# Filters' loop of a hybrid attention and Hyena kernel: token transpositions moved and paired, a fourth PSUM bank from the eighth step

## The chip, the cores and the metric

One core of one Trainium2 chip. The metric is the time of an execution in microseconds, as the device reports it; three runs of the kernel before took 1793.38, 1794.36 and 1795.69 us. One further execution was taken with the profiler: 1791.72 us, of which 1789.9 us are the span that the trace covers. The change touches one loop, which takes about a tenth of the span.

## The reference, cut to what matters

The reference is a backbone of two layers over 1024 latent tokens and 256 context tokens of width 1024: an attention layer, then a Hyena layer, then a final RMSNorm.

```
h_lat = rms_norm(x_lat, norm_w[0]) * (1 + scale) + shift        # 1024 tokens
h_ctx = rms_norm(x_ctx, norm_w[0]) * (1 + scale_c) + shift_c    # 256 tokens
attention over h_lat, h_ctx: (h @ w_in) split into queries, keys, values, gate ...
# odd layer
h    = sin-MLP(positions) @ w3 + b3, times exp(-t * |deltas|)   # filters: 2 orders, 2 directions, 1024 channels
kern = [fwd, 0, reversed bwd];  kern = kern / sum |kern|
k_f  = rfft(kern)                                               # the spectrum that the long convolutions multiply by
```

The loop that is changed does two things that do not depend on each other. It computes the filters' spectrum k_f for the Hyena layer (by two stages of matrix products in place of an FFT), and in its gaps it prepares the attention layer's input: each of 10 tiles of 128 tokens (2 of context, 8 latent) is scaled by its reciprocal norm, transposed, modulated, and split into a high and a low part for products of nearly full precision.

## The kernel before

Instructions of TensorE (PE), VectorE (DVE), ScalarE (ACT) and GpSimd (POOL) are written out by hand: each engine runs them in the order of the program text. DMA issues on SyncE (SP) are not: their order is made when the kernel is built, by when buffers are expected free, and an issue can stand far ahead of its place in the text.

The filters' loop (L615) has 38 steps, n = 0 to 37. Steps 0 to 31 each take one of 32 parts (8 groups p of 128 channels, 4 parts each); the later stages trail behind: the first stage one step (`first_stage(n - 1, .)`), the second stage and the copies of spectra six steps. In the text a step is, in order:

- `taps(n)`: eight products into a two-bank PSUM tile `pw` (L483, L484)
- `second_stage(.., 0)`: products of the regrouped first-stage results `au` (L583) into one bank `pq`
- `decayed(n)`: DVE multiplies the taps by the decay, tile `kern` (L541)
- `decay(n + 1, .)`: ACT's exponentials for the next step (L536), whose one buffer `dec` is free when `kern` is done
- `spectra(.., 0)`: DVE scales the second stage's bank into `kc` (L594), and a DMA stores it to `Kd`
- `first_stage(n - 1, 0 and 1)`: a product of `sum` or `dif` (L568) and ACT's copy to `aT` (L569), one half after the other, the decays between them
- `halves(n)`: GpSimd's sum and difference of `kern`'s halves (L561); `norms(n)`: DVE's reduction of absolute values `kabs` (L548) and GpSimd's addition (L552)
- `second_stage(.., 1)`, `regroup` (DMAs from `aT` to `au`, L578), `spectra(.., 1)`: the second `kc`
- every fourth step: the sum over partitions (L649) and its reciprocal `rn` (L661), n = 5, 9, 13, ...; the split of the next coefficients (`split_coefs`: L345 and L348 on ACT, L346 on GpSimd, L349 on DVE), n = 2, 6, 10, ...
- at the end of a step, generators are pulled: `row_stats` (the tiles' norms, up to step 11), then `xprep` (the tokens, steps 11 to 32), and `first_products` (steps 32 to 35).

`xprep` (L392) handles half a tile (four blocks of 128 columns) per step. One pull issues four transpositions into a bank `pq` (L414); the next, directly behind, issues four activations on ACT that scale and shift into `raw` (tile `mraw`, L419), the castings to the high part on DVE (L426) and the subtractions that give the low part on GpSimd (L427). Context tiles have one 128x512 casting per half, latent tiles two of 128x256. At the start of a tile DVE scales all of it (L408), every second step, and the next tile's load is issued (L399), into one of two `xt` buffers.

`pq()` hands out PSUM banks in rotation: a product waits until the reader of the bank's last use is done. At first three banks rotate, since the fourth, "c", serves the modulation's products early in the loop; it is put into the rotation at the end of step 19.

`first_products` are the first blocks of the attention layer's input projection: 12 products of 128x288 per pull. Their weights are loaded at step W1N = 22 into the buffer `ckh`, split at step 24 into `ckl` and `kpe` (L678 on ACT, L679 on GpSimd), and the next part of the weights is loaded into `ckh` at step 26 (L682). In the last group of channels the stores of `kc` are issued by ACT. Behind the loop the remaining first products and all other chunks of the projection follow; their weights are split on ACT (L742) and GpSimd (L743), and ACT's part stands in its queue behind the stores of `kc`.

The token section's core, of before:

```
            nc.vector.tensor_scalar(xt, xt, rr[:, t:t + 1], 0.0, ALU.mult, ALU.add)
            load()
            for k0 in (0, 4):
                yield
                ps = pq()
                for i in range(4):
                    nc.tensor.transpose(ps[:, i * P:(i + 1) * P], xt[:, (k0 + i) * P:(k0 + i + 1) * P], ident)
                yield
```

Of the kernel before, what the change touches and what calls it, by code (L numbers as in the profile page):

```python
# [9 lines left out]
F32 = mybir.dt.float32  # L10
# [7 lines left out]
P = 128  # L18
# [22 lines left out]
W1N = 22  # L41
HP = {32: 1, 33: 1, 34: 1, 35: 1}
# [62 lines left out]
def f(ap):  # L105
    return ap.bitcast(F32)


def backbone(tc, I, out):
# [12 lines left out]
    def nm(s):  # L122
        cnt[0] += 1
        return f"{s}_{cnt[0]}"
# [9 lines left out]
    def pq():  # L134

        t = banks.popleft()
        banks.append(t)
        return bank(t)
# [253 lines left out]
    def xprep():  # L392

        xts = []

        def load():
            if len(xts) < NC + NT:
                xt = pre.tile([P, D], F32, tag="xt", bufs=2, name=nm("xt"))
                nc.sync.dma_start(xt, xsrcs[len(xts)])  # L399
                xts.append(xt)  # L400

        load()
        yield
        for t in range(NC + NT):
            who, t0 = ("x", t * P) if t < NC else ("l", (t - NC) * P)
            A, Sh = ada[who, 0, "scale"], ada[who, 0, "shift"]
            xt = xts[t]
            nc.vector.tensor_scalar(xt, xt, rr[:, t:t + 1], 0.0, ALU.mult, ALU.add)  # L408
            load()
            for k0 in (0, 4):  # L410
                yield
                ps = pq()
                for i in range(4):
                    nc.tensor.transpose(ps[:, i * P:(i + 1) * P], xt[:, (k0 + i) * P:(k0 + i + 1) * P], ident)  # L414
                yield
                raw = pre.tile([P, 4, P], F32, tag="mraw", bufs=2, name=nm("mraw"))
                for i in range(4):
                    k = k0 + i
                    nc.scalar.activation(raw[:, i], ps[:, i * P:(i + 1) * P], AF.Identity, bias=Sh[:, k:k + 1], scale=A[:, k:k + 1])  # L419
                if who == "x":  # L420
                    dst = [((hxh[:, k0:k0 + 4, t0:t0 + P], hxl[:, k0:k0 + 4, t0:t0 + P]), raw)]
                else:
                    th, c = divmod(t0, 512)
                    dst = [([h0[th, k0 // 2 + j, i][:, :, c:c + P] for i in range(2)], raw[:, 2 * j:2 * j + 2]) for j in range(2)]
                for (hi, lo), r in dst:
                    nc.vector.tensor_copy(hi, r)  # L426
                    nc.gpsimd.tensor_tensor(lo, r, f(hi), ALU.subtract)  # L427
# [7 lines left out]
    def pull(g, n=1):  # L435
        for _ in range(n):
            next(g, None)
# [3 lines left out]
    with tc.manual_schedule(engines=ENG):  # L441
# [173 lines left out]
        for n in range(N + 6):  # L615
# [9 lines left out]
            pb, ub = divmod(n - 6, 4)  # L625
            if 0 < n < N:
                taps(n)
            if n >= 6:
                ps0 = second_stage(pb, ub, 0)
            if n < N:  # L630
                decayed(n)
            decay(n + 1, 0)
# [7 lines left out]
            if n < N:  # L640
                halves(n)
                norms(n)
            if n >= 6:
                ps1 = second_stage(pb, ub, 1)
# [29 lines left out]
            if 12 < n < 33:  # L674
                pull(toks, 2)
            if n == W1N + 2:
                for k in range(4):
                    nc.scalar.copy(w0[1][:, k], w0[0][:, k])  # L678
                    nc.gpsimd.tensor_tensor(w0[2][:, k], w0[0][:, k], f(w0[1][:, k]), ALU.subtract)  # L679
            if n == W1N + 4:  # L680
                w1 = ckp.tile([P, KEYS], F32, tag="ckh", bufs=1, name=nm("w0"))[:, :4 * 288].rearrange("p (k n) -> p k n", k=4)
                nc.sync.dma_start(w1, win[:, 4:8, 0:288])  # L682
            pull(first_products, HP.get(n, 0))
            if n == 19:
                banks.append("c")
# [1628 lines left out]
```

## Time and profile before

| what | value |
|---|---|
| three runs | 1793.38, 1794.36, 1795.69 us |
| profiled execution | 1791.72 us |
| its span in the trace | 1789.9 us |
| steps 12 to 31 of the loop, start of kern to start of kern | 95.65 to 223.80 us of the span |
| tail of the loop | about 229 to 251 us |
| busy share of the span | PE 95%, DVE 63%, POOL 47%, ACT 42% |

A row of the order of time gives start and length in microseconds, the engine ("q" behind it: its queue of DMA issues), the line, the operation, what it writes and reads, the shape, and a count when equal ones follow each other; in brackets stands how long the engine sat idle before it and what ended that. A grouped row gives the count, the busy time in us and the mean in ns of one, and the idle time before them with what ended it. Lengths of neighbours on DVE overlap by some 0.08 us, so sums are made from start to start.

### The profile page before, as it was taken

The page shows a single profiled execution, that of the slowest core. Times are in us where ns is not written, and L with a number is a line of the kernel's source. Part 1 is how long each engine was busy: PE and PEld are TensorE (multiplying, and loading weights), DVE is VectorE, ACT ScalarE, POOL GpSimd, SP SyncE. Part 2 cuts the span into 40 slices and gives each one's busy share as a digit, 9 for nine tenths or more (in the row PEclk, how much of TensorE's full clock was granted, in tenths as well). Part 3 has the DMA queues.
Part 4 walks back from the last instruction along what each step waited for, and adds up shares of the span by engine and source line. Part 5 has one row for each costly group of instructions (what it writes and reads, how often), then busy time and mean ns, then how long its engine had stood idle before and what let it go on. Part 6 is the DMA issues. An engine that isn't in the chain of part 4 may idle for free. (4 is left out here: it accounts for less than half of the span.)

```text
span 1789.9 us, 25447 instructions
## 1 busy us (share of the span) xinstructions
PE 1698.6 (95%) x9360; PEld 1313.9 (73%) x9360; DVE 1136.4 (63%) x1625; ACT 751.7 (42%) x1293; POOL 837.1 (47%) x612
## 2 busy tenths in 40 slices
PE   6888899998999999999999999999999999999898
PEld 2555588986766666666666788888888888878786
DVE  6888957636666665466665324556777667756843
ACT  4766621243545545644444333233333333333331
POOL 3667832524179877677777453123222223233300
PEclk8999999999999999999999999999999999999999
DMA  7776787322220010100010226456776666686432
GB/s 258 243 217 200 211 260 266 110 71 72 57 57 28 11 44 14 52 31 24 22 34 22 78 94 161 138 152 203 199 213 174 196 201 196 196 231 181 155 108 104
DMA packets 237372, 236.48 MB, mean 132 GB/s; under 512 B 30575, under 2 KB 195223, under 8 KB 236831
## 3 DMA queue, kind: packets, MB, share of 16 engines
q1 hardware_dynamic: 235072, 232.76, 43.6%
q10 hardware_dynamic: 2176, 2.10, 0.4%
q8 instruction: 74, 1.21, 0.3%
q14 instruction: 50, 0.41, 0.1%
HBM read 152.87 MB, written 61.94 MB: 120 GB/s over the span
## 5 line engine op out<-in xcount | busy, mean ns | idle before, releaser
L1010 DVE TENSOR_REDUCE mx<-pq 128x1 f32<-128x512 f32 x256 | 170.9, 682 | 100.4 <-PE pq L1009 98.6
L1315 ACT ACTIVATE PT<-pw 128x1024 f32<-128x1024 f32 x160 | 163.6, 1025 | 166.1 <-PE pw L1297 160.1
L100 PE MATMUL pw<-h1h,wh 128*128 128x512 f32 x512 | 208.4, 407 | 0.0
L102 PE MATMUL pw<-h1h,wl 128*128 128x512 f32 x512 | 201.3, 393 | 0.0
L101 PE MATMUL pw<-h1l,wh 128*128 128x512 f32 x512 | 200.0, 391 | 0.0
L1209 POOL TENSOR_TENSOR acc<-acc,PT 128x1024 f32<-128x1024 f32 x62 | 147.4, 2378 | 20.4 <-ACT PT L1315 18.9
L1733 POOL TENSOR_TENSOR wl<-wr,wh 128x1024 fp32r<-128x1024 f32 x32 | 77.1, 2409 | 137.8 <-ACT wh L1732 127.5
L102 PEld LDWEIGHTS pw<-h1h,wl 128*128 128x128 f32 x512 | 96.1, 188 | 21.3
L101 PEld LDWEIGHTS pw<-h1l,wh 128*128 128x128 f32 x512 | 96.5, 188 | 17.7
L100 PEld LDWEIGHTS pw<-h1h,wh 128*128 128x128 f32 x512 | 96.5, 188 | 17.4
L1868 POOL TENSOR_TENSOR K<-K,skp 128x512 f32<-128x512 f32 x32 | 42.7, 1337 | 122.7 <-DMA K<-Kd 121.7
L1207 POOL TENSOR_TENSOR acc<-PT,PT 128x1024 f32<-128x1024 f32 x31 | 74.0, 2386 | 52.5 <-ACT PT L1315 49.8
L1881 DVE TENSOR_TENSOR cA<-pq,K 64x512 f32<-64x512 f32 x128 | 88.1, 689 | 1.8
L1877 DVE SCALAR_TENSOR_TENSOR cB<-pq,K 64x512 f32<-64x512 f32 x64 | 44.4, 693 | 70.4 <-PE pq L1874 35.6
L1848 ACT COPY caT<-pq 128x512 f32<-128x512 f32 x64 | 37.6, 588 | 118.1 <-PE pq L102 98.1
L583 PE MATMUL pq<-au,FBk 128*128 128x256 f32 x256 | 71.6, 408 | 14.8 <-DVE kc L594 11.1
L1894 PEld LDWEIGHTS pq<-cA,GB 128*128 128x128 f32 x512 | 67.3, 193 | 15.3 <-issue 10.3
L1200 PE MATMUL pv<-PT,Va 128*64 128x256 f32 x640 | 77.9, 385 | 0.0
L1896 ACT COPY cbT<-pq 128x512 f32<-128x512 f32 x64 | 37.5, 587 | 95.7 <-PE pq L1894 67.1
L1200 PE MATMUL pv<-PT,Vm 128*64 128x256 f32 x640 | 77.7, 385 | 0.0
L1894 PE MATMUL pq<-cA,GB 128*128 128x128 f32 x512 | 68.8, 278 | 7.9 <-DVE cA L1884 6.9
L1911 DVE TENSOR_TENSOR cil<-spare,cih 128x512 fp32r<-128x512 f32 x64 | 53.8, 879 | 34.8 <-ACT cih L1910 34.6
(448 smaller groups left out, 4672.6 us busy)
## 6 DMA issues: line engine op xcount, KB each, us to landing
au<-aT SPq DMA_DIRECT2D x128, 128.0 KB
space<-in_ada_w_dram SPq DMA_DIRECT2D x32, 512.0 KB
wr<-in_hy_w_in_dram SPq DMA_DIRECT2D x32, 512.0 KB
K<-Kd SPq DMA_DIRECT2D x64, 256.0 KB
ad<-caT SPq DMA_DIRECT2D x64, 256.0 KB
cau<-ad SPq DMA_DIRECT2D x32, 512.0 KB
bd<-cbT SPq DMA_DIRECT2D x32, 512.0 KB
spare<-bd SPq DMA_DIRECT2D x64, 256.0 KB
```

What stands on the lines that cost most here:

```text
L100: nc.tensor.matmul(ps, lh, rh, start=start, stop=False)
L101: nc.tensor.matmul(ps, lh, rl, start=False, stop=False)
L102: nc.tensor.matmul(ps, ll, rh, start=False, stop=stop)
L583: nc.tensor.matmul(ps[:, i * CB:(i + 1) * CB], FBk[:, 4 * uc + 2 * j + i, :], aus[p, uc][:, 2 * j + i, :], start=True, stop=True)
L1010: nc.vector.reduce_max(m[:, i, j:j + 1], ps, axis=AX.X)
L1200: nc.tensor.matmul(ps[64 * e:64 * e + 64, 0:256], vals[:, 2 * s + j], PT[:, j, 256 * e:256 * e + 256], start=s == 0 and j == 0, stop=s == ...
L1207: eng.tensor_tensor(accs[gi], prev, PT, ALU.add)
L1209: eng.tensor_tensor(accs[gi], accs[gi], PT, ALU.add)
L1315: nc.scalar.activation(PT, ps.rearrange("p (a q) -> p a q", q=512), AF.Exp, scale=SC_A if kind == 0 else SC_M)
L1733: nc.gpsimd.tensor_tensor(wl, f(r), f(wh), ALU.subtract)
L1881: nc.vector.tensor_tensor(A1[64 * e:64 * e + 64], pv[64 * e:64 * e + 64], K[:, 0], ALU.mult)
L1894: nc.tensor.matmul(ps[:, i * P:(i + 1) * P], GB[:, 4 * uc + i, :], A1[:, i, :], start=True, stop=True)
```

## The change

`xprep` works on pairs of tiles. A step now takes two blocks of 128 columns of both tiles of a pair: four transpositions into one bank, two activations of 128x256, one casting and one subtraction of 128x512, for context and latent tiles alike. The work of a step is pulled in four pieces at four places of its text: the transpositions ahead of the taps; the activations behind kern and ahead of the next decays; casting and subtraction behind the halves and ahead of the norms; and, behind the norms, once per pair, the next loads and the scaling of the next two tiles. In DVE's queue the casting so stands between the first kc and kabs, and the scalings between kabs and the second kc.

The loads are no longer two buffers deep. Five tiles are asked for at step 11, and three of the ten go through `ckh`, `ckl` and `kpe`, two more through `ckl` and `kpe` later. The first weights therefore move: their load is written at step 26 in place of 22, their split at step 32 (24), the second load at step 34 (26), and the first products are pulled in steps 33 to 36 (32 to 35). The bank "c" joins the rotation at the end of step 6 in place of 19.

```
-W1N = 22
-HP = {32: 1, 33: 1, 34: 1, 35: 1}
+W1N = 26
+XT = ("xt", "xt") + CK + ("xt", "xt", "ckl", "xt", "kpe")
+LN = 2, 1, 2, 0, 0
+HP = {33: 1, 34: 1, 35: 1, 36: 1}
...
+        def scaled(t):
+            for i in range(t, min(t + 2, NC + NT)):
+                nc.vector.tensor_scalar(xts[i], xts[i], rr[:, i:i + 1], 0.0, ALU.mult, ALU.add)
+
+        load(5)
         yield
-        for t in range(NC + NT):
+        scaled(0)
+        yield
+        for t in range(0, NC + NT, 2):
...
+            for k0 in range(0, NK, 2):
+                ps = pq()
+                for k in range(2):
+                    for i in range(2):
+                        nc.tensor.transpose(ps[:, (2 * k + i) * P:(2 * k + i + 1) * P], xts[t + i][:, (k0 + k) * P:(k0 + k + 1) * P], ident)
                 yield
+                raw = pre.tile([P, 4, P], F32, tag="mraw", bufs=2, name=nm("mraw")).rearrange("p (k i) c -> p k (i c)", k=2)
+                for k in range(2):
+                    kk = k0 + k
+                    nc.scalar.activation(raw[:, k], ps[:, 256 * k:256 * k + 256], AF.Identity, bias=Sh[:, kk:kk + 1], scale=A[:, kk:kk + 1])
                 yield
...
+                nc.vector.tensor_copy(hi, raw)
+                nc.gpsimd.tensor_tensor(lo, raw, f(hi), ALU.subtract)
+                yield
+                if k0 == NK - 2:
+                    load(LN[t // 2])
+                    scaled(t + 2)
+                yield
...
+            tokens = 12 < n < 33
+            if tokens:
+                pull(toks)
             if 0 < n < N:
                 taps(n)
             if n >= 6:
                 ps0 = second_stage(pb, ub, 0)
             if n < N:
                 decayed(n)
+            if tokens:
+                pull(toks)
             decay(n + 1, 0)
...
             if n < N:
                 halves(n)
+            if tokens:
+                pull(toks)
+            if n < N:
                 norms(n)
+            if tokens:
+                pull(toks)
...
-            if 12 < n < 33:
-                pull(toks, 2)
-            if n == W1N + 2:
+            if n == W1N + 6:
...
-            if n == W1N + 4:
+            if n == W1N + 8:
...
-            if n == 19:
+            if n == 6:
                 banks.append("c")
```

`load(n_)` issues the next n_ tiles' loads, each into the buffer that `XT` names.

More of the change, by code (lines that the diff above doesn't have):

```diff
@@ L394, in xprep, with load @@
         xts = []
[L396 to L399, printed above, removed]
+        def load(n_):
+            for t in range(len(xts), min(len(xts) + n_, NC + NT)):
+                tag = XT[t]
+                xt = (pre.tile([P, D], F32, tag=tag, bufs=2, name=nm("xt")) if tag == "xt" else
+                      ckp.tile([P, KEYS], F32, tag=tag, bufs=1, name=nm("xt"))[:, :D])
+                nc.sync.dma_start(xt, xsrcs[t])
@@ L400, in load @@
                 xts.append(xt)
-        load()
+        def scaled(t):
+            for i in range(t, min(t + 2, NC + NT)):
+                nc.vector.tensor_scalar(xts[i], xts[i], rr[:, i:i + 1], 0.0, ALU.mult, ALU.add)
+        load(5)
         yield
-        for t in range(NC + NT):
+        scaled(0)
+        yield
+        for t in range(0, NC + NT, 2):
             who, t0 = ("x", t * P) if t < NC else ("l", (t - NC) * P)
             A, Sh = ada[who, 0, "scale"], ada[who, 0, "shift"]
[L407 to L410, printed above, removed]
+            for k0 in range(0, NK, 2):
[3 more added lines that the diff above has]
+                        nc.tensor.transpose(ps[:, (2 * k + i) * P:(2 * k + i + 1) * P], xts[t + i][:, (k0 + k) * P:(k0 + k + 1) * P], ident)
@@ L411, in xprep @@
                 yield
-                ps = pq()
-                for i in range(4):
-                    nc.tensor.transpose(ps[:, i * P:(i + 1) * P], xt[:, (k0 + i) * P:(k0 + i + 1) * P], ident)
+                raw = pre.tile([P, 4, P], F32, tag="mraw", bufs=2, name=nm("mraw")).rearrange("p (k i) c -> p k (i c)", k=2)
+                for k in range(2):
+                    kk = k0 + k
+                    nc.scalar.activation(raw[:, k], ps[:, 256 * k:256 * k + 256], AF.Identity, bias=Sh[:, kk:kk + 1], scale=A[:, kk:kk + 1])
@@ L415, in xprep @@
                 yield
[L416 to L419, printed above, removed]
                 if who == "x":
-                    dst = [((hxh[:, k0:k0 + 4, t0:t0 + P], hxl[:, k0:k0 + 4, t0:t0 + P]), raw)]
+                    hi, lo = (x[:, k0:k0 + 2, t0:t0 + 256] for x in (hxh, hxl))
@@ L422, in xprep @@
                 else:
                     th, c = divmod(t0, 512)
[L424 to L427, printed above, removed]
+                    hi, lo = (h0[th, k0 // 2, i][:, :, c:c + 256] for i in range(2))
+                nc.vector.tensor_copy(hi, raw)
+                nc.gpsimd.tensor_tensor(lo, raw, f(hi), ALU.subtract)
```

## The prediction

> **What bounds the kernel now.** I read the page first, then the filters' loop in windows of four steps (one group of 128 channels: the loop repeats with that period), then the groups of instructions inside it, and at last the order of time of VectorE and GpSimd.
>
> ```profile
> span 1789.9 us, 25447 instructions
> ```
>
> The windows below are cut at starts of the row "kern" (L541), one per step: steps 14 to 17, 18 to 21, 22 to 25, 26 to 29, and then the tail from the first product of step 32 to the first product behind the loop. The columns are the length, then busy time (count) of PE, PEld, DVE, ACT and POOL, the granted clock, the DMA share and GB/s.
>
> ```profile
> 107.72:136.07 28.35, 23.99 (x99) 16.64 (x100) 23.21 (x27) 17.19 (x46) 19.47 (x18) 0.88 0.67 195
> 136.07:163.63 27.56, 23.65 (x101) 16.16 (x102) 24.29 (x30) 17.00 (x46) 20.30 (x22) 0.94 0.69 205
> 163.63:190.86 27.23, 23.57 (x100) 15.72 (x101) 25.14 (x30) 18.14 (x50) 23.35 (x26) 0.94 0.69 202
> 190.86:217.55 26.69, 22.24 (x99) 15.16 (x98) 24.64 (x31) 16.83 (x46) 20.29 (x22) 0.94 0.71 214
> 228.75:251.36 22.61, 22.37 (x136) 20.37 (x135) 10.58 (x15) 3.53 (x9) 3.70 (x6) 1.00 0.85 245
> ```
>
> In the loop DVE is busy 23.2 to 25.1 of about 27 us and is the engine that the others wait for. In the tail PE is busy 22.37 of 22.61: there PE sets the end, and behind it the products go on without a pause, so what the loop and the tail gain or lose is what the kernel gains or loses.
>
> VectorE, from the middle of step 26 to the start of step 28 (start, length, engine, line, operation; in brackets the idle time before it and what ended it):
>
> ```profile
> 194.53 0.68 DVE L594 TENSOR_TENSOR kc<-pq,rn 128x512 f32<-128x512 f32 x1
> ...
> 196.74 0.53 DVE L349 TENSOR_TENSOR WB<-b3r,WB 1x256 fp32r<-1x256 f32 x1 [0.33 <-ACT WB L348]
> 197.44 0.29 DVE L426 CAST h<-mraw 128x256 fp32r<-128x256 f32 x1 [0.17 <-ACT mraw L419]
> ...
> 198.67 0.74 DVE L408 TENSOR_SCALAR xt<-xt,rr 128x1024 f32<-128x1024 f32 x1
> 199.33 1.21 DVE L541 TENSOR_TENSOR kern<-pw,dec 128x1024 f32<-128x1024 f32 x1
> ```
>
> ```profile
> 200.47 0.68 DVE L594 TENSOR_TENSOR kc<-pq,rn 128x512 f32<-128x512 f32 x1
> 201.06 2.02 DVE L548 TENSOR_REDUCE kabs<-kern 128x256 f32<-128x1024 f32 x1
> 203.00 0.68 DVE L594 TENSOR_TENSOR kc<-pq,rn 128x512 f32<-128x512 f32 x1
> 203.60 0.45 DVE L426 CAST h<-mraw 128x256 fp32r<-128x256 f32 x1
> 204.30 0.70 DVE L426 CAST h<-mraw 128x256 fp32r<-128x256 f32 x1 [0.25 <-ACT mraw L419]
> 204.92 1.21 DVE L541 TENSOR_TENSOR kern<-pw,dec 128x1024 f32<-128x1024 f32 x1
> ```
>
> From start to start, step 27 spends 1.14 on kern, 0.59 on the first kc, 1.94 on kabs, 0.60 on the second kc, 4.27 in all, and then 1.32 on two token castings. Step 26 has the castings from 197.27 (their wait included) to 198.67, 1.40. The same stretch on GpSimd:
>
> ```profile
> 200.69 1.28 POOL L561 TENSOR_TENSOR sum<-kern 128x512 f32<-128x512 f32 x1 [0.69 <-DVE kern L541]
> 201.92 1.29 POOL L561 TENSOR_TENSOR dif<-kern 128x512 f32<-128x512 f32 x1
> 203.16 0.73 POOL L552 TENSOR_TENSOR kabs<-kabs,kabs 128x256 f32<-128x256 f32 x1
> 204.13 0.73 POOL L427 TENSOR_TENSOR h<-mraw,h 128x256 fp32r<-128x256 f32 x1 [0.23 <-DVE h L426]
> ```
>
> This is what the forecast rests on. A casting with GpSimd idle takes 0.29 (197.44). The one at 203.60 meets the running kabs sum, which ends at 203.89, and ends 0.16 behind it; the one at 204.30 meets a subtraction that ends at 204.86 and ends 0.14 behind it. A casting that starts while a GpSimd operation runs does not end before that operation has. The kabs reduction (201.06) runs beside both halves and takes its usual time.
>
> **The change part by part.**
>
> *Castings.* Forty tile halves become twenty blocks of 128x512, one per step: 36 castings become 20. What a double one costs with GpSimd idle is the second row here, and the first the present form with its waits in:
>
> ```profile
> L426 DVE CAST h<-mraw 128x256 fp32r<-128x256 f32 x30 | 12.5, 429 | 5.1 <-ACT mraw L419 5.1
> L426 DVE CAST hxh<-mraw 128x512 fp32r<-128x512 f32 x4 | 1.6, 411 | 3.9 <-ACT mraw L419 3.9
> L427 POOL TENSOR_TENSOR hxl<-mraw,hxh 128x512 fp32r<-128x512 f32 x4 | 5.9, 1477 | 7.8 <-DVE hxh L426 7.8
> ```
>
> The waits for ACT (5.1 and 3.9) go, because transposition and activation now stand a good part of a step ahead. But the casting now stands behind the first kc, at the place of 201.06, where the sum half runs until 201.97. It then ends about 0.28 later (0.16 as above and 0.12 for the double width), at 202.25, and kabs can start at 202.17: 1.11 us per step where 0.41 would be the cost with GpSimd idle. Bounds: 0.34 (0.41 less the usual overlap of starts) and 2.4 (it also loses its turn to the dif half, 1.29). I take 1.11.
>
> *Scalings.* Before, one tile every second step at 0.74; now two at once every fourth step, behind kabs. GpSimd's queue has then sum, dif (pushed to 202.2 to 203.5) and the low parts, 1.48 wide form, until about 205; kabs ends near 204.1. If a scaling waits like a casting, the first ends at about 205.5, the kabs addition (0.73) takes its turn, and the second ends near 206.7: 2.6 for the pair. If not, 2 x 0.74 = 1.48. These are the bounds, and I take 2.6, since it is the castings' case. [...] No scaling of the trace of before starts under a running GpSimd operation.
>
> *Other parts of a cycle.* The reciprocal stays, 1.76. The coefficients' split waits for ACT's chain, which hangs on kern: its second part starts at 196.74, 5.88 behind that step's kern (190.86). Now the second kc starts at 3.67 + 1.11 = 4.78 and ends its turn at 5.38, the split ends at about 6.4 as before: 1.1 instead of 2.1 (195.13 to 197.27). So the later kc is hidden in this one step of four. A cycle: 4 x 4.27 + 4 x 1.11 + 1.76 + 2.6 + 1.1 = 27.0. The four cycles measured make 109.83; four of 27.0 make 108: **-1.8**, nearly all in the first cycle.
>
> *Transpositions first.* The same 80 on PE, moved ahead of the taps. PE has 22.2 to 24.0 us of work in a cycle of 27, so they cost nothing while DVE is this slow; below 24 PE would be next. Activations: two of 128x256 instead of four of 128x128; ACT is busy 17 of 27. Hidden by kern's wait, in either form. The low parts: one of 1.48 for two of 0.73, GpSimd is busy 20 of 27, hidden.
>
> *Fourth bank from step 7.* It can only take away waits of PE for kc and of DVE for PE. Of these DVE felt
>
> ```profile
> 71.26 1.23 DVE L541 TENSOR_TENSOR kern<-pw,dec 128x1024 f32<-128x1024 f32 x1 [0.64 <-PE pw L484]
> ```
>
> ```profile
> L583 PE MATMUL pq<-au,FBk 128*128 128x256 f32 x256 | 71.6, 408 | 14.8 <-DVE kc L594 11.1 <-ACT mraw L419 2.5 <-DMA au<-aT 1.2
> ```
>
> The first row is worth **-0.6** (0 to -0.9); PE's waits for kc, in the second, are idle time of an engine that is not the bound there.
>
> *Loads.*
>
> ```profile
> 44.77 0.38 SPq L624 DMA_DIRECT2D w<-in_w_in_dram  x1
> ```
>
> SP issues as soon as a buffer is free, not in step order: the weight load written at step 22 went out at 44.77. So the three token tiles in ckh, ckl and kpe go out there as well, 1.5 MB instead of 0.58; at 240 to 260 GB/s that is 4 us more in the queue ahead of the first au. PE waited 1.2 us for au in the whole loop: cost 0 (to 3). Scaling now needs tiles 0 and 1 at the end of step 12:
>
> ```profile
> 98.12 0.40 SPq L596 DMA_DIRECT2D Kd<-kc  x1
> 98.62 0.41 SPq L399 DMA_DIRECT2D xt<-in_ctx_dram  x1
> ...
> 99.84 0.74 DVE L408 TENSOR_SCALAR xt<-xt,rr 128x1024 f32<-128x1024 f32 x1
> ...
> 102.50 0.69 DVE L594 TENSOR_TENSOR kc<-pq,rn 128x512 f32<-128x512 f32 x1 [0.79 <-DMA Kd<-kc]
> ```
>
> The second scaling adds **+0.7**. The store issued at 98.12 frees its buffer at 102.5, so tile 1, issued behind it at 98.62, lands near 102.9; DVE wants it at 100.5. If its place in SP's queue stays, that is a wait of 2.4; if it moves up with its step, 0. I take **+1.0**.
>
> *Tail.*
>
> ```profile
> 228.22 1.10 PE L568 MATMUL pq<-dif,FKc 128*128 128x512 f32 x2 [0.18 <-DVE kc L594]
> 230.38 0.38 PE L100 MATMUL pw<-w,hxh 128*128 128x288 f32 x1
> 232.05 1.89 PE L583 MATMUL pq<-au,FBk 128*128 128x256 f32 x8
> 239.53 1.97 PE L583 MATMUL pq<-au,FBk 128*128 128x256 f32 x8 [0.24 <-DMA au<-aT]
> ```
>
> The last first-stage product waits for the last kc (0.18), which now stands behind a casting: up to 0.9 later. One block of first products (230.38 to 232.05, 1.67) no longer fills the wait for au ahead of 239.53: PE comes there 1.67 earlier and waits up to that much more. And the second weight load (576 KB; 2.4 us at 245 GB/s), which used to pass in the loop, now goes out when the split of step 32 is done, among the last au. Bounds 0 and 4.9; I take **+2.5**.
>
> Sum: -1.8 - 0.6 + 0.7 + 1.0 + 2.5 = **+1.8 us**. The profiled execution took 1791.72 around its span of 1789.9, so 1793.5; the median of the runs, 1794.36, lies 2.64 above that execution, so **1796.2** is what I expect of a median. Own range of this case 1793 to 1801.
>
> **The rivals.**
>
> *A. The castings do not wait for GpSimd* (they slip in ahead of the sum half, or the sum starts late). Then a casting costs 0.41, the scalings 1.48, and a cycle 4 x 4.68 + 1.76 + 1.48 + 2.1 = 24.1, which is just above PE's work. That is 2.9 less in each of four cycles and some 0.8 in the last steps: 1796.2 - 12.4 = 1784. For it: the waits for ACT do end, and two of the four steps have no other use for the time. Against it: every casting above that met a GpSimd operation ended behind it, and the sum starts 0.15 behind kern each time.
>
> *B. The tail decides* (slower). Here the loop comes out as forecast, but the second weight load passes in front of the last au and the missing block adds its full time: +4.9 instead of +2.5, with tile 1's full wait of 2.4: 1796.2 + 3.8 = 1800; with au late at the loop's start too, 1803. It decides from the point where PE idles over 2 us between step 32 and the first product behind the loop. For it: DMA is at 0.85 there, the highest of the five windows. Against it: SP may hold the load back.
>
> *C. The castings wait for both halves*, 2.4 each: 20 x 1.29 = 26 more, 1822; in one step of four, 1803. Against it: 203.60 ended right behind one operation.
>
> *D. Nothing changes* because VectorE's sum of work is the same and all else is hidden: 1794.
>
> **How the numbers follow.** Forecast 0.45, A 0.27, B 0.15, C 0.08, D 0.05. A measurement of this kernel can tell about 0.2%, 3.6 us, from no change. Faster by more: nearly all of A and a little of the forecast's lower end, 0.29. Slower by more: a third of the forecast, most of B and C, 0.35. Between: 0.36. The range from 1781 to 1804 takes in A, B, and C where it is rare.
>
> **What would show it.** In the new profile the casting (x20, 128x512) starts inside the sum half and lasts near 1.1 us, not 0.41; the waits for ACT ahead of it are gone; the scalings' pairs take 2.6; the step with the split is shorter, that with the reciprocal longer; a cycle is near 27; PE idles more between step 32 and the chunk. [...]

## The result, and the profile after

The changed kernel takes 1806.76 us (median of 5, 1806.32 to 1811.29), the kernel before in the same comparison 1793.38 us: the comparison puts the ratio at 1.009, 95% interval 1.0071 to 1.0109 (the two medians alone give 1.0075). It is slower by 13.4 us where I forecast 1796.2, and outside my range. The profiled spans stand 1804.9 to 1789.9, so the traces have 15.0 us to account for.

The same cut into cycles of four steps as in the prediction, at kern of steps 13, 17, 21, 25 and 29 (length, then busy time of PE, PEld, DVE, ACT and POOL, granted clock, DMA share, GB/s), in the changed kernel:

```profile
106.84:135.49 28.65, 23.05 (x99) 16.32 (x98) 25.87 (x25) 15.12 (x38) 19.26 (x17) 0.92 0.63 192
135.49:163.73 28.24, 22.71 (x99) 15.89 (x98) 25.84 (x25) 15.12 (x38) 19.26 (x17) 0.92 0.64 190
163.73:192.56 28.83, 23.22 (x99) 16.03 (x98) 25.93 (x26) 15.12 (x38) 19.26 (x17) 0.91 0.62 193
192.56:221.22 28.66, 23.06 (x99) 16.16 (x98) 25.88 (x25) 15.12 (x38) 19.27 (x17) 0.92 0.57 165
```

I had forecast 27.0. DVE is busy 25.9 and PE 23, so neither is full: in each cycle DVE stands still for more than 2 us. VectorE in order of time, step 16 and the start of step 17, shows where:

```profile
126.22 1.21 DVE L553 TENSOR_TENSOR kern<-pw,dec 128x1024 f32<-128x1024 f32 x1
127.35 0.68 DVE L606 TENSOR_TENSOR kc<-pq,rn 128x512 f32<-128x512 f32 x1
127.95 1.17 DVE L433 CAST hxh<-mraw 128x512 fp32r<-128x512 f32 x1
129.05 1.92 DVE L560 TENSOR_REDUCE kabs<-kern 128x256 f32<-128x1024 f32 x1
130.87 1.82 DVE L408 TENSOR_SCALAR xt<-xt,rr 128x1024 f32<-128x1024 f32 x2
132.61 0.68 DVE L606 TENSOR_TENSOR kc<-pq,rn 128x512 f32<-128x512 f32 x1
135.49 1.22 DVE L553 TENSOR_TENSOR kern<-pw,dec 128x1024 f32<-128x1024 f32 x1 [2.20 <-PE pw L496]
```

kern waits 2.20 for the taps (pw). TensorE over the same moment shows why the taps are late:

```profile
132.18 0.30 PE L421 MATMUL pq<-ident,xt 128*128 128x128 f32 x1 [3.77 <-DVE xt L408]
...
133.30 0.56 PE L495 MATMUL pw<-WA,HA 128*128 128x256 f32 x1
133.66 0.41 PE L496 MATMUL pw<-WB,HB 128*128 128x256 f32 x1
133.87 0.41 PE L495 MATMUL pw<-WA,HA 128*128 128x256 f32 x1
```

The transpositions of step 17 are first in PE's queue and wait 3.77 for a tile that VectorE scales only at the end of step 16. The taps need nothing from that tile, but they stand behind it, and kern needs the taps. So VectorE waits for PE, which waited for VectorE. The same wait stands at kern of step 13, behind the first scalings, and of steps 21, 25 and 29:

```profile
102.64 1.40 DVE L408 TENSOR_SCALAR xt<-xt,rr 128x1024 f32<-128x1024 f32 x2
106.84 1.22 DVE L553 TENSOR_TENSOR kern<-pw,dec 128x1024 f32<-128x1024 f32 x1 [2.80 <-PE pw L496]
...
163.73 1.23 DVE L553 TENSOR_TENSOR kern<-pw,dec 128x1024 f32<-128x1024 f32 x1 [2.20 <-PE pw L496]
...
192.56 1.22 DVE L553 TENSOR_TENSOR kern<-pw,dec 128x1024 f32<-128x1024 f32 x1 [1.80 <-PE pw L496]
...
221.22 1.22 DVE L553 TENSOR_TENSOR kern<-pw,dec 128x1024 f32<-128x1024 f32 x1 [2.20 <-PE pw L496]
```

With step 17 that is 11.2 us.

The whole difference, in sections cut at kern's starts and at the first product behind the loop (PE `pw<-wh,hxh`, 251.36 before), in us:

| from | to | before | after | difference |
|---|---|---|---|---|
| kern 1 | kern 6 | 23.9 | 24.9 | +1.0 |
| kern 6 | kern 11 | 31.1 | 32.9 | +1.9 |
| kern 11 | kern 13 | 10.2 | 13.6 | +3.5 |
| kern 13 | kern 31 | 123.3 | 126.1 | +2.8 |
| kern 31 | first product | 27.6 | 32.6 | +5.0 |
| first product | end | 1538.6 | 1539.3 | +0.8 |

The first row need not be the change: two kernels below that are the kernel before in these steps take 24.9 and 24.8 there, and five variants with the changed kernel's text there take 23.9 to 24.3.

### The profile page after: what moved, and what is told of

Its sections match the earlier page's. It is cut to its first block, busy times and chain, and to the rows that moved or that the text cites. A ratio compares the mean times of both kernels' runs of the same rounds, so it can differ in the third digit from the quotient of the medians.

```text
span 1804.9 us, 25367 instructions
## 1 busy us (share of the span) xinstructions
PE 1703.1 (94%) x9360; PEld 1317.9 (73%) x9360; DVE 1138.5 (63%) x1609; ACT 742.1 (41%) x1253; POOL 831.3 (46%) x596
```

## The experiments

Theory Q, formed from the comparison above: the taps, queued behind transpositions that wait for a late scaling, cost the loop's gain and more; the castings cost what I had forecast; early loads and the tail make up the rest. Rivals: the castings or the loads set the time and the wait is only where it shows; the tail comes from late stores and not from the weights. The same sections in all kernels, with the ratio to the kernel before as each one's own comparison gives it ("product" is the first product behind the loop, which the expectations also call the first product of the second half):

| kernel | 6 to 11 | 11 to 13 | 13 to 31 | 31 to product | product at | ratio |
|---|---|---|---|---|---|---|
| before | 31.1 | 10.2 | 123.3 | 27.6 | 251.4 | |
| after | 32.9 | 13.6 | 126.1 | 32.6 | 265.5 | 1.0090 |
| a_taps_first | 34.5 | 10.8 | 121.8 | 31.9 | 258.7 | 1.0053 |
| a_scale_early | 32.7 | 13.7 | 122.3 | 32.2 | 260.4 | 1.0055 |
| a_cast_late | 34.0 | 14.3 | 120.3 | 31.5 | 259.5 | 1.0043 |
| a_tf_cl | 33.3 | 10.8 | 111.9 | 31.9 | 247.3 | 1.0004 |
| a_both | 32.5 | 13.6 | 119.5 | 30.5 | 255.2 | 1.0040 |
| a_load_late | 29.8 | 15.0 | 130.1 | 32.1 | 267.3 | 1.0087 |
| a_loads | 30.9 | 13.2 | 126.9 | 32.3 | 262.6 | 1.0073 |
| b_bank6 | 31.2 | 10.1 | 121.0 | 27.8 | 250.2 | 1.0000 |
| b_tail | 30.9 | 10.2 | 121.5 | 31.0 | 253.8 | 1.0008 |
| b_hp33 | 30.1 | 10.2 | 122.3 | 29.4 | 251.4 | 1.0009 |
| b_w1late | 31.0 | 10.2 | 121.8 | 30.3 | 252.9 | 1.0027 |
| c_best | 31.2 | 13.1 | 112.1 | 31.8 | 247.4 | 0.9985 |
| c_w1_32 | 32.2 | 13.2 | 111.3 | 31.0 | 247.7 | 0.9991 |
| c_w1_34 | 28.5 | 14.9 | 115.1 | 31.2 | 249.9 | 0.9987 |

What follows the first product took 1537.0 to 1544.4 us in these profiles, without a pattern I can name; so sections are read from the traces, and ratios only where they are clear of that. A section of a single profile varies too, where the text is the same: steps 13 to 31 take 123.3 in the kernel before and 122.3 in b_hp33, which is the same there (121.0 to 121.8 in the other b kernels); steps 6 to 11 take 32.5 to 34.5 in the changed kernel and the five variants with its early loads, and 28.5 to 32.2 in the three c kernels. So a difference below 2 us between two profiles in these two sections, and below 4 in the c kernels' steps 6 to 11, is not told from chance.

### The queue: a_taps_first and a_scale_early

```diff
-            if tokens:
-                pull(toks)
             if 0 < n < N:
                 taps(n)
             if n >= 6:
                 ps0 = second_stage(pb, ub, 0)
+            if tokens:
+                pull(toks)
```

> The changed kernel, but a step's four transpositions stand behind its taps and its first second-stage product on TensorE; castings, bank, loads and scaling as changed. Theory Q (queue): the taps stood behind transpositions that wait for the scaling, which VectorE does at the end of the step before; so the product kern of steps 13, 17, 21, 25 and 29 no longer waits for the taps (2.80, 2.20, 2.20, 1.80 and 2.20 us in the changed kernel, 11.2 in all). Of that some 0.77 us per cycle comes back, because the casting of those steps then meets GpSimd's sum again (1.19 us instead of 0.42): about -7 us, 1800 us (1797 to 1802). Rival C (castings and loads set the time, the wait only shows where VectorE is early): steps 13 to 31 keep their length, 1805 to 1808 us.

Measured: 1801.87 us, ratio 1.0053 (1.0037 to 1.0069). No kern waits for taps any more; the three full cycles from step 17 on, by the same columns:

```profile
133.07:159.81 26.74, 21.58 (x100) 14.35 (x100) 26.54 (x27) 15.22 (x38) 19.49 (x17) 1.00 0.70 201
159.81:187.60 27.79, 22.93 (x100) 15.82 (x99) 26.86 (x27) 14.99 (x38) 19.46 (x17) 0.94 0.68 204
187.60:214.33 26.73, 21.57 (x100) 14.36 (x99) 26.53 (x26) 15.11 (x38) 19.48 (x17) 1.00 0.61 176
```

DVE is busy 26.5 of 26.7: it is the bound again. TensorE in step 17 of this kernel:

```profile
129.47 0.28 PE L496 MATMUL pw<-WB,HB 128*128 128x256 f32 x1
129.59 0.28 PE L495 MATMUL pw<-WA,HA 128*128 128x256 f32 x1
...
132.04 0.30 PE L421 MATMUL pq<-ident,xt 128*128 128x128 f32 x1 [1.19 <-DVE xt L408]
```

The transposition still waits for the scaling, 1.19, but now nothing that VectorE needs soon stands behind it. The first product behind the loop comes 6.8 us earlier. Rival C (castings and loads) falls for these 7 us.

```diff
+                if k0 == NK - 4:
+                    scaled(t + 2)
                 if k0 == NK - 2:
                     load(LN[t // 2])
-                    scaled(t + 2)
```

> The changed kernel, but a pair of token tiles is scaled one step earlier (at the end of the third step of a cycle of four, not of the fourth); the transpositions stay first on TensorE, everything else as changed. Theory Q (queue): the scaling is a whole step ahead of the transposition that needs it, so kern of steps 17, 21, 25 and 29 no longer waits for the taps (2.20, 2.20, 1.80, 2.20 = 8.4 us; step 13's 2.80 stays), 0.77 us of each comes back by a longer casting: about -5.5 us, 1801 us (1798 to 1804). Rival C (castings and loads): the scaling only changes places, 1805 to 1808 us. Rival O (order alone): even a ready transposition ahead of the taps delays kern; waits of over 1 us stay and the time is 1804 to 1807 us.

Measured: 1801.59 us, ratio 1.0055 (1.0039 to 1.0071); the waits at steps 17, 21, 25 and 29 are gone, that of step 13 (2.80) stands, the product comes 5.2 us earlier. Transpositions ahead of the taps make no kern wait where their tile is ready, so rival O falls too: what cost these 8.4 us of waits is the late input at the head of TensorE's queue.

### The castings: a_cast_late

```diff
             if n < N:
                 halves(n)
-            if tokens:
-                pull(toks)
-            if n < N:
                 norms(n)
...
                 spectra(pb, ub, 1, ps1)
+            if tokens:
+                pull(toks)
```

(In the token generator the scaling goes ahead of the casting, so that it keeps its place.)

> The changed kernel, but the casting of a step (with its low part) stands at the end of VectorE's step, behind the second spectrum copy, where GpSimd has done its sum; transpositions, scaling, bank and loads as changed. Theory L (the casting pays for GpSimd's running sum): the 14 castings of 1.17 to 1.22 us come down to about 0.45, some -10 us; the waits of kern for the taps stay, and the scaling is followed by one casting more, so they are shorter rather than longer: 1797 us (1794 to 1801). Rival W (the width of the casting is its price): it stays at 1.2 us, 1805 to 1809 us. Rival P (TensorE sets the cycle): castings of 0.45 us but the waits of kern grow by as much, 1804 to 1808 us.

Measured: 1799.65 us, ratio 1.0043 (1.0025 to 1.0062). A casting of the changed kernel and GpSimd's sum beside it, in order of time on each engine:

```profile
115.04 1.27 POOL L573 TENSOR_TENSOR sum<-kern 128x512 f32<-128x512 f32 x1 [1.01 <-DVE kern L553]
115.41 1.19 DVE L433 CAST hxh<-mraw 128x512 fp32r<-128x512 f32 x1
137.28 0.42 DVE L433 CAST h<-mraw 128x512 fp32r<-128x512 f32 x1
```

The casting starts inside the sum, which ends at 116.31, and ends at 116.60, 0.29 behind it; the one at 137.28, in a step where kern and so the sum were late, took 0.42. With the casting at the end of the step, where only the short kabs sum runs:

```profile
126.09 0.72 POOL L564 TENSOR_TENSOR kabs<-kabs,kabs 128x256 f32<-128x256 f32 x1
126.43 0.67 DVE L437 CAST hxh<-mraw 128x512 fp32r<-128x512 f32 x1
```

All but one of the twenty castings now take 0.41 to 0.67. Width is not the price (rival W), the GpSimd instruction that happens to run is. The taps' waits stayed (2.81, 1.87, 1.58, 1.54, 0.74), so rival P falls.

### Both moves: a_tf_cl and a_both

a_tf_cl has the edits of a_taps_first and a_cast_late, a_both those of a_scale_early and a_cast_late.

> Both moves at once: the transpositions behind the taps and the first second-stage product, and the casting at the end of VectorE's step; scaling, bank, loads and tail as in the changed kernel. Theory Q with L: with the transpositions moved alone a steady cycle of four steps is 26.9 us (152.78 to 179.69), all of it VectorE at work; four castings of some 0.55 instead of 1.19 us take 2.5 off: cycles of 24.4 us, the stretch from kern of step 13 to kern of step 31 some 111 us (121.8 with the transpositions moved alone, 123.3 before), 1789 us (1786 to 1793), so a little faster than the kernel before. Rival P (TensorE, or the Kd stores, become the bound below 26 us): waits for PE or for DMA show up at kern or kc, the stretch stays above 117 us and the time is 1794 to 1798 us.

Measured: the section from 13 to 31 is 111.9 us, as theory Q with L has it (111), against 123.3 before. Its cycles:

```profile
129.91:154.56 24.65, 21.30 (x99) 14.35 (x98) 23.32 (x27) 15.13 (x39) 19.01 (x17) 1.00 0.74 222
154.56:180.13 25.57, 21.24 (x99) 14.35 (x98) 23.37 (x26) 14.98 (x39) 18.98 (x17) 1.00 0.72 213
180.13:204.22 24.09, 21.05 (x99) 14.35 (x98) 23.40 (x27) 15.13 (x39) 19.02 (x17) 1.00 0.71 222
```

So the change's own parts, in another order on two queues, take 11.4 us off steps 13 to 31 (9.1 against the shortest b kernel). The time is 1792.23 us, ratio 1.0004 (0.9989 to 1.002), that of the kernel before and above the 1789 I expected: the start and the tail keep 7.1 us of it (2.2, 0.6 and 4.3 in the table's sections), and behind the first product, which comes 4.1 us earlier than before, the profile is 2.3 us longer, which I cannot explain.

> The scaling one step earlier and the casting at the end of VectorE's step; the transpositions stay first on TensorE, all else as in the changed kernel. Theory Q with L: with the scaling moved alone a steady cycle is 27.5 us (154.93 to 182.49), in which the scaled pair takes 2.23 us and the castings 1.2; with castings of some 0.55 it is 25 us; kern of step 13 still waits 2.8 us: 113 to 115 us from kern of step 13 to kern of step 31, 1791 us (1788 to 1795). Rival O (a transposition ahead of the taps costs of itself, since it waits for what the step before does last): the waits of kern for the taps come back at over 0.5 us, 1795 to 1800 us.

Measured: 1798.1 us, ratio 1.004 (1.0026 to 1.0055), and 119.5 us for the section: my figure was too low, and by neither theory: the time lies in rival O's range, but its sign, waits of kern, stayed away. No kern but that of step 13 waits for taps; kc waits for its stores instead, on VectorE, as here in step 16:

```profile
132.85 0.69 DVE L607 TENSOR_TENSOR kc<-pq,rn 128x512 f32<-128x512 f32 x1 [2.84 <-DMA Kd<-kc]
```

and SP shows two token loads, 1 MB, just ahead of the stores:

```profile
123.72 0.95 SPq L403 DMA_DIRECT2D xt<-in_x_dram  x2
125.34 0.38 SPq L609 DMA_DIRECT2D Kd<-kc  x1
128.12 0.38 SPq L609 DMA_DIRECT2D Kd<-kc  x1
```

With cycles near 25 us the bunching of transfers may be the next limit; that these two loads are the cause was not tried by itself.

### The early loads: a_load_late

```diff
+                if t in (2, 3, 4):
+                    nc.vector.memset(xt[:, 0:1], 0.0)
                 nc.sync.dma_start(xt, xsrcs[t])
```

> The changed kernel, but the loads of token tiles 2, 3 and 4 can't start before step 11: VectorE writes a zero into the first column of each buffer there, and the load has to come behind it; all else as changed. Theory B (burst): the three loads at 45.8 and 49.7 us make the statistics' tiles and the first regrouping loads late; kern of step 6 to kern of step 11 takes 31.1 to 31.7 us as in the kernel before (31.09) and with the bank alone (31.21), instead of 32.9 to 34.5 in the changed kernel and its three variants: 1.3 to 3 us less, 1804.5 us (1802 to 1806.5). Rival: the steps 6 to 10 come out over 32.7 us again, and it is the later scaling or the statistics themselves; 1806 to 1808 us.

Measured: 1807.49 us, ratio 1.0087 (1.007 to 1.0103). In the changed kernel SP issues

```profile
45.76 0.38 SPq L403 DMA_DIRECT2D xt<-in_x_dram  x1
48.70 0.33 SPq L381 DMA_DIRECT2D xs<-in_x_dram  x1
49.72 0.83 SPq L403 DMA_DIRECT2D xt<-in_x_dram  x2
53.98 2.93 SPq L590 DMA_DIRECT2D au<-aT  x4
```

and with the three token loads held back steps 6 to 11 take 29.8 us instead of 32.9: theory B is right for this section. But five loads then go out together at 92.6 to 97.0, PE waits for au in step 13,

```profile
107.96 2.05 PE L597 MATMUL pq<-au,FBk 128*128 128x256 f32 x4 [2.89 <-DMA au<-aT]
```

and the later sections lose 5.3 us (11 to 31). The burst was moved, not spread, and the time is that of the changed kernel, as the rival had it.

### The bank: b_bank6

```diff
-            if n == 19:
+            if n == 6:
                 banks.append("c")
```

> The kernel before with one edit: the fourth bank is used from the eighth step instead of from the twenty-first. By the steps of the two traces (steps 7 and 8: 4.94 and 5.13 us before, 4.22 and 4.45 in the changed kernel) it takes 1.4 us from these two steps and some tenths from the later ones: 1791.5 us (1790 to 1793). Rival: the short steps come from what was late ahead of them and not from the bank: within 0.1% of the kernel before, steps 7 and 8 as before.

Measured: 1792.98 us, ratio 1.0 (0.9988 to 1.0013). kern's wait of 0.64 at 71.26 is gone and steps 7 and 8 take 9.14 instead of 10.07 us, but steps 9 and 10 take 1.0 more, and step 6 to 11 comes out as before (31.2 and 31.1). TensorE waits there for a regrouping load, which an earlier start does not bring sooner:

```profile
83.59 1.10 PE L583 MATMUL pq<-au,FBk 128*128 128x256 f32 x4 [3.66 <-DMA au<-aT]
```

I had expected 1.4 and more to remain; the rival was right on the time, though steps 7 and 8 did change.

### The tail: b_tail, b_hp33 and b_w1late

In the kernel before, the weights' part of the change:

```diff
-HP = {32: 1, 33: 1, 34: 1, 35: 1}
+HP = {33: 1, 34: 1, 35: 1, 36: 1}
-            if n == W1N + 2:
+            if n == W1N + 10:
-            if n == W1N + 4:
+            if n == W1N + 12:
```

> The kernel before with the weights' part of the change alone: the first weights are split at the end of step 32 instead of 24, the second load of weights stands behind step 34 instead of 26, and the first half of the products starts in step 33 instead of 32; tokens, castings and bank as before. Theory T (missing filler and a late second load): from kern of step 31 to the first product of the second half takes 31.5 to 32.5 us, as in the changed kernel and its variants (31.5 to 32.6), instead of 27.6 before: 1796.5 us (1795 to 1798). Rival K (the changed kernel's tail is late by its last casting and by stores of kc that go out late, not by the weights): 27.5 to 28.7 us, 1792 to 1793.5 us.

Measured: 1794.17 us, ratio 1.0008 (0.9993 to 1.0024); the section grows from 27.6 to 31.0, a little under theory T; the time lies between the two ranges and, with 1 inside its interval, decides nothing. From kern of step 31 to the end of the last copy of aT it is 6.14 us in both kernels; all of the 3.4 lies behind that copy (21.42 and 24.82; b_bank6, with the tail of before, has 21.64). The two halves of it, each alone in the kernel before: b_hp33 has the new `HP` and nothing else, b_w1late this:

```diff
-            if n == W1N + 4:
+            if n == W1N + 12:
                 w1 = ckp.tile([P, KEYS], ...
+                nc.vector.memset(w1[:, :, 0:1], 0.0)
```

> The kernel before with the first half of the products starting in step 33 instead of 32, nothing else. Both weight loads and the split stay where they are. If the missing block is what lengthens the tail, from the last copy of aT to the second half of the products it takes 23.1 us or more instead of 21.42 (one block is 1.67 us of TensorE), up to the 24.82 of the kernel with both halves: 1793 to 1796 us. If the late load is, 21.4 to 22 us and the time of the kernel before.

> The kernel before with the second load of weights alone behind step 34: VectorE writes a zero into its first columns there, so that it can't start sooner; products from step 32, split as before. If the late load among the last transfers is what lengthens the tail, from the last copy of aT to the second half of the products it takes 23.5 to 24.8 us instead of 21.42, 1793 to 1796 us. If the missing block is, 21.4 to 22 us and the time of the kernel before.

Measured: 23.22 us behind the last aT without the block of step 32 (1793.75 us, ratio 1.0009, 0.9997 to 1.002), 24.10 with the late load (1795.75 us, ratio 1.0027, 1.0016 to 1.0039). The late load alone, SP and then the next VectorE wait:

```profile
242.77 0.38 SPq L683 DMA_DIRECT2D w<-in_w_in_dram  x1
```

```profile
248.78 0.69 DVE L594 TENSOR_TENSOR kc<-pq,rn 128x512 f32<-128x512 f32 x1 [3.53 <-DMA Kd<-kc]
```

and without the block, TensorE:

```profile
237.40 1.97 PE L583 MATMUL pq<-au,FBk 128*128 128x256 f32 x8 [1.50 <-DMA au<-aT]
```

Both halves cost: 1.8 for the missing block (1.67 of products no longer fill PE's wait for au, which is 1.50 here and was 0.24 before), 2.7 for the load among the last stores, and 3.4 together, since they partly cover one another. Rival K falls for these 3.4: the last stores are late, but the load of the weights makes them so. The changed kernel's tail has 1.1 more ahead of the last aT (7.25 instead of 6.14) and 3.9 behind it; 0.5 of the 3.9 has no cause shown. There the load goes out behind the last load of au and the last store that SP issues (254.21):

```profile
254.85 0.44 SPq L702 DMA_DIRECT2D w<-in_w_in_dram  x1
```

VectorE's last kc then wait 1.54, 2.52 and 0.34 for stores, where those of the kernel before wait 1.01, 0.43 and 0.29.

### Other orders of the loads: a_loads, c_best, c_w1_32, c_w1_34

One edit, made to a_tf_cl (c_best) and to the changed kernel (a_loads); with it the split of the first weights moves to step 29, the second load to step 30 and `HP` back to step 32:

```diff
-XT = ("xt", "xt") + CK + ("xt", "xt", "ckl", "xt", "kpe")
+XT = (CK + ("xt", "xt")) * 2
+TL = {9: 1, 10: 1, 11: 1, 13: 1, 14: 1, 16: 1, 17: 1, 20: 1, 21: 1, 24: 1}
...
+            token_load(TL.get(n, 0))
```

> Transpositions behind the taps and the first second-stage product, castings at the end of VectorE's step, and another order of the token loads and buffers: tiles 0, 1 and 2 go into the three weight buffers, held back until the ends of steps 9, 10 and 11 by a zero that VectorE writes into their first column, the others follow one load per step (steps 13, 14, 16, 17, 20, 21, 24); with that the weight buffers are free after step 28, the first weights are split at the end of step 29, the second load of weights stands behind step 30, and the first half of the products starts in step 32 as in the kernel before. Theory: the parts add. Step 6 to 11 about 30 us (29.75 with the loads held, 33.3 with the two moves alone), step 13 to 31 about 112 us (111.9 with the two moves), from kern of step 31 to the first product of the second half 27.6 to 28.5 us (27.56 before, 31.9 with the two moves): the second half of the products starts near 241 us instead of 247.3 with the two moves and 251.4 before, 1783 us (1779 to 1788). Rival (the transfers of a shorter loop bunch up, or PE has idle time that the later parts take back): a section stays 2 us or more over its figure, 1787 to 1792 us.

Measured: 1792.11 us, ratio 0.9985 (0.9973 to 0.9997): the only kernel whose interval lies below 1, by less than the 0.2% that I called tellable, and 9 us above my figure. Step 6 to 11 gained 2.1 over a_tf_cl and step 11 to 13 lost 2.3 again; the gain is within the spread of that section, the loss stands in all three c kernels (13.1 to 14.9 against 10.8). Behind the last aT the tail is 21.87 as hoped, but that copy now comes 9.94 us behind kern of step 31: the rival's case.

> The changed kernel with the order of its token loads, buffers and weights alone as in c_best; transpositions first on TensorE, castings behind the first spectrum copy, scaling and bank as changed. Theory: step 6 to 11 about 30 us instead of 32.95, from kern of step 31 to the first product of the second half 28 to 29 us instead of 32.6 (the last casting and its step keep up to 1 us), the five waits of kern for the taps stay: 7 us less than the changed kernel, 1799.5 us (1797 to 1803). Rival K (the tail comes from the late stores of kc and not from the weights): the tail stays over 31 us, 1803 to 1805 us.

Measured: 1806.85 us, ratio 1.0073 (1.0056 to 1.0091). Step 6 to 11 is near the figure (30.9), but the last aT comes 9.66 us behind kern 31, so the tail gains almost nothing and stays over 31 us, as rival K had it; the product comes 2.9 us earlier, behind it the profile is 3.0 longer, and my figure was 7 us too low. In c_best SP at that place:

```profile
212.89 0.38 SPq L702 DMA_DIRECT2D w<-in_w_in_dram  x1
213.37 0.45 SPq L608 DMA_DIRECT2D Kd<-kc  x1
```

A kc waits 1.52 for a store at 218.28. I took the 576 KB just ahead of a store for the cause and moved that load in the code (`n == W1N + 5` to `W1N + 7` and `W1N + 9`), to step 32 and to step 34:

> c_best with the second load of weights behind step 32 instead of step 30; the first products still start in step 32. In c_best the 576 KB go out at 212.89 us, just ahead of a store of kc (213.37); kern of step 31 to the last copy of aT then takes 9.94 us, against 6.7 with the two moves alone, and from that copy to the second half of the products 21.87, against 25.19. Theory S (the load ahead of the store makes kc, then PE late): behind step 32 the load meets neither the last two steps' stores nor their kc: 6.7 us to the last aT, and then, if the missing products were what made the tail long, 21.9 us: 28.6 us in all, the second half of the products at 244 us, 1789 us (1785 to 1792). Rival M (the split of the first weights at step 29 and the products in step 32 are what delays the last steps): 9.5 to 10 us to the last aT, as c_best, 1791 to 1794 us.

> c_best with the second load of weights behind step 34, where the changed kernel has it; the first products still start in step 32. It tells the two halves of the tail apart. If the missing block of products is what the changed kernel's tail lacks, the last aT to the second half of the products stays near 21.9 us although the load is late; if the late load among the last regrouping loads is what costs, it is 24.3 to 25.3 us again, as in the changed kernel and in the kernel before with the weights' part alone. Kern of step 31 to the last aT 6.7 us by theory S (9.5 to 10 by rival M). With products as the cause 28.6 us and 1789 us (1785 to 1792); with the load as the cause 31.5 us and 1792 us (1789 to 1795).

Measured: 1791.44 us, ratio 0.9991 (0.9978 to 1.0004), and 1790.7 us, ratio 0.9987 (0.9974 to 1.0). Neither tells theory S from rival M: the load went out at 214.06 and 216.07, at the same place in SP's queue, ahead of the same store, and the last aT came 8.28 and 8.22 us behind kern 31. What makes that copy late in these kernels stays open; the two halves of the tail were told apart by b_hp33 and b_w1late instead.

## Why the prediction was wrong

*Castings: right.* Forecast 1.11 per step in place of 0.41, since a casting ends about 0.28 behind the running sum; found 1.17 to 1.22, ending 0.29 behind it, except in the steps that the taps made late. Steps without another use come to 5.37 where 4.27 + 1.11 makes 5.38. Rival A, with castings of 0.41, did not hold. With the casting at another place it takes 0.41 to 0.67 in all but one (a_cast_late), and with the transpositions moved too the cycles, 24.1 to 25.6 (a_tf_cl), come near A's 24.1.

*Scalings: they wait for GpSimd, but the size was too high.* Forecast 2.6 for a pair, my estimate from the castings; 1.82 in step 16 (130.87), and 1.40 in step 12 (102.64), where no GpSimd instruction runs. So a scaling that starts under a running one took longer, as the castings did. But the pair of step 16 met one running instruction, a low part that ends at 131.47, and not two:

```profile
130.21 1.26 POOL L434 TENSOR_TENSOR hxl<-mraw,hxh 128x512 fp32r<-128x512 f32 x1
```

My 2.6 had the kabs addition take its turn between the two scalings, as in step 27. But `norms` has no addition in the first step of a group, and the pairs stand in steps 16, 20, 24 and 28, which are first steps. In a_scale_early, where the pair stands one step earlier and meets an addition, it takes 2.23; no run shows 2.6.

*Splits: too low.* 1.1 forecast, 1.8 found from the second kc's turn to kern at 120.85:

```profile
118.44 0.68 DVE L606 TENSOR_TENSOR kc<-pq,rn 128x512 f32<-128x512 f32 x1
119.14 1.67 DVE L351 TENSOR_TENSOR WB<-b3r,WB 1x256 fp32r<-1x256 f32 x2
120.85 1.23 DVE L553 TENSOR_TENSOR kern<-pw,dec 128x1024 f32<-128x1024 f32 x1
```

This and the scalings cancel, by luck: the cycle without the queue is 26.7 to 27.8 (a_taps_first) against 27.0 forecast. Steps 13 to 31 take 1.5 less there than before, against 1.8, but the b kernels, without the changed token steps, take 121.0 to 122.3, so that gain is not shown.

*"Transpositions first ... cost nothing while DVE is this slow": this step failed.* I compared PE's busy time with DVE's and did not ask, as one must of an instruction that can wait, what stands behind it on its engine and who waits for that. The scaling's row (`xt<-xt,rr`) and the transposition's (`pq<-ident,xt`) were both in my working; that the one is the last thing of a step and the other now the first of the next was not put together. It cost 11.2 us of kern's waits, less what shorter castings gave back: 6.8 us by a_taps_first. The cycles came to 28.2 to 28.8 with neither PE nor DMA full: PE was busy 22.7 to 23.2 us of them, DMA at a share of 0.57 to 0.64.

*Start of the tokens.* Forecast +0.7 for the second scaling and +1.0 for tile 1. The pair took 1.40, so the first is right; tile 1 was there in time in the changed kernel, and the 2.80 of that step are the taps' wait.

*Loads: 0 (to 3), found 1.9* in steps 6 to 11; the six kernels with these early loads take 32.5 to 34.5 there, the five with the loads of before 30.1 to 31.2. I looked at PE's waits for au in the kernel before (1.2), which says nothing of a queue with 1 MB more in it.

*Fourth bank: -0.6, found nothing* that remains, though the wait it was to remove went.

*Tail: +2.5 (0 to 4.9), found +5.0.* The missing block and the late load both cost, 1.8 and 2.7, 3.4 together. But the load does not go out among the last au, as I and rival B had it: it goes out behind them, and what it makes late is the last stores of kc. 1.1 more is the kc that stands behind a casting, forecast as up to 0.9: in a_cast_late, with the casting behind kc, the last aT comes 6.15 behind kern 31 again. So rival B's place and size were right and its way was not; with the loop as I had it, it would have made 1796.2 + 2.5, some 1799.

In sum the forecast of +1.8 misses by 13.2 of 15.0: some 7 from the queue, 2.5 from the tail, 1.9 from the loads, 1.0 from a start that varies from kernel to kernel, the rest in pieces under 1.

## What to carry to other kernels

When work is moved to the front of an engine's queue, don't ask only whether the engine has time for it: ask when its input is ready, what stands behind it, and who needs that. Here the same transpositions behind the taps, or with a scaling one step earlier, give the loop its length of before. A casting of VectorE's that started under GpSimd's sum, or under its short kabs sum, ended 0.29 us behind it in these traces (1.17 to 1.22 long under the first, 0.67 under the second at 126.09, 0.42 at 109.06 with none running), so its place in the step was worth more than its width: castings moved behind the long sums and transpositions behind the taps took steps 13 to 31 from 123.3 to 111.9 us, though start and tail gave most of that back and the kernel's time stayed as before. In b_w1late a bulk load issued among the last stores made late the buffers that they free (2.7 us of the tail), and SP issued a load far from where it is written: written at steps 32 and 34, it went out ahead of kern of step 31 (c_w1_32, c_w1_34).

## What the runs showed of the hardware that I had not expected

Behind the wait at the head of TensorE's queue the taps were slow too. After the 3.77 us of standing still the taps start every 0.21 us (133.66 to 133.87 above); in a_taps_first every 0.12 (129.47 to 129.59), so eight taps cost some 0.75 more. The window around it, in the changed kernel, has a granted clock of 0.67:

```profile
131.00:136.00 5.00, 3.55 (x14) 3.21 (x15) 2.80 (x4) 1.02 (x2) 0.48 (x1) 0.67 0.59 182
```

With both moves the cycles run at 1.00 and PE's busy time for the same 99 matmuls falls from 23 to 21.2. But TensorE was slow without a wait of that length as well: in a_scale_early, behind a wait of 2.54, four products of au take 1.91 (at 156.60) where they take 1.02 at 160.02, and the kernel before has four stretches at a clock of 0.50 between 116 and 206 us with no wait of PE longer than 1.92. Ahead of one of them PE was busy 1.54 of 3.40:

```profile
144.20:147.60 3.40, 1.54 (x7) 1.02 (x7) 3.40 (x4) 1.74 (x6) 2.71 (x3) 1.00 0.57 177
147.60:151.00 3.40, 3.40 (x15) 3.19 (x14) 2.63 (x5) 2.00 (x6) 2.72 (x4) 0.50 0.69 204
```

So slow taps alone don't set the changed kernel apart from the kernel before; what sets the granted clock, these runs don't show.

The wait between VectorE and GpSimd went both ways in a_scale_early: where the pair of scalings starts under GpSimd's low part, the pair takes 2.23, and GpSimd's kabs sum, 0.72 to 0.73 in the steps without a scaling, takes 1.17:

```profile
151.46 1.27 POOL L434 TENSOR_TENSOR h<-mraw,h 128x512 fp32r<-128x512 f32 x1
152.18 2.23 DVE L408 TENSOR_SCALAR xt<-xt,rr 128x1024 f32<-128x1024 f32 x2
152.69 1.17 POOL L565 TENSOR_TENSOR kabs<-kabs,kabs 128x256 f32<-128x256 f32 x1
```
